# Moving the S5 blocks' rows between partitions by DMA through DRAM, in a two-layer decoder trunk on one core

## The chip, the cores and the metric

The kernel runs on one core of a Trainium2 chip. The metric is the time of one execution on the device in microseconds (us). The kernel before took 1357.15 us (median of three runs, 1355.7 to 1358.05). A profile is one execution recorded by the hardware profiler. Its engines are TensorE (PE, with its weight loads as PEld), VectorE (DVE), ScalarE (ACT), GpSimd (POOL) and SyncE (SP). "SPq" and "ACTq" are DMA issues by SP and ACT.

## The reference, cut to what matters

One sequence of 512 tokens, width 1024, passes two layers; each has a token mixer and a SwiGLU feed-forward part. The first layer's mixer has two branches on the same normalised input, an S5 state space and an HGRN2 recurrence, whose outputs are concatenated and projected. Only the S5 branch is touched:

```python
uf = u.reshape(bsz, seq, S5_GROUPS, 16)             # 32 groups of 16 channels, 64 complex states each
bu = einsum('gph,blgh->blgp', b_bar, uf)
_, states = associative_scan(combine, (a, bu), axis=1)       # state_t = lam_bar * state_{t-1} + bu_t
y = einsum('ghp,blgp->blgh', c_mat, states).real + d_skip * uf
y = gelu(y.reshape(bsz, seq, 512))
y_a = y * sigmoid(y @ w_glu + b_glu)                 # S5 branch
y_b = hgrn2_mixer(hq, hf, hi, hg, ...)               # four heads of 128
mixed = concatenate([y_a, y_b]) @ ev_w_out
```

## The kernel before

All activations lie with channels on the 128 partitions and the 512 tokens along the free dimension. Products are made with fp32 split into a high and a low float32r part (`split`, `wsplit`: an ACT copy makes the high part, a subtraction on DVE the low part) and three matmuls for each pair (`proj`, lines 275 to 277). Weights come by SP's DMA queue into three "raw" buffers. The adaLN products (`ada_run`) run beside all this: SP loads pieces of `ada_w` into two "ar" buffers, and DVE adds each to `acc` (L202, L204); these additions keep their program order on DVE, and `pace` says how many go with each weight load.

The S5 branch has 512 channels, in four blocks of 128 (`s5_block(q, ...)`, q = 0 to 3). Its input is `ups[q]`, the projection `u`, which lies in PSUM, in one of four "mm" buffers; the same four buffers serve the later projections. The block takes four consecutive tokens at a time, so that the recurrence steps over 128 groups of four. For that, rows have to change partition. U[32r..32r+31, j, n] (r = 3 - s) is channel 32j..32j+31 of token 4n + s: token phase s moves to a quarter of the partitions, and channel quarter j moves to the free dimension. Sixteen DVE copies of 32 partitions by 128 do this (L775). Then PE makes `vps` from `U` (L780), DVE and POOL rotate it (the tiles `rz0a` to `rz0d`, with q as the digit), DVE scans (L792), both rotate back, and PE makes `yp` (L804 to L806), again with token phases on the partition quarters. Sixteen ACT copies of 32 by 128 put `yp` back into channel order as `yf`.

`s5_next()` calls one block, and then `s5_mats(q + 1)` prepares the next block's matrices: products on POOL, copies into zeroed tiles on ACT, small transposes on PE. The four calls stand between the HGRN2 heads' projections (`hg_fq`, `hg_v`, `hg_g`: tiles hq, hf, hk, lg, hv, hg) and their recurrence cores (`core`: tiles e_h, sc_h, tot_h, lv_h). When all four `yf` are there, `gelu()` runs on each in place and `s5_glu` splits them, multiplies by `s5_w_glu`, and gates (`ys`). ACT's functions that need a table run in program order (`tact`), so the sigmoids of head 3 come after the last gelu.

Working tiles come from pools with tags, each with a number of slots: "s" has 16, "X" 4, "r" 8. Five "s" slots stay with the zeroed tiles. `U` takes an "X" slot for q below 3 and an "s" slot for q = 3; `yf` takes an "r" slot. The order of the instructions on each engine is not the written one: a planner chooses it, by the priority of the program order and its own costs, when a tile's slot and inputs are there. At run time each engine goes through its list in order.

Of the kernel before, what the change touches and what calls it, by code (L numbers as in the profile page):

```python
# [8 lines left out]
F32 = mybir.dt.float32  # L9
# [4 lines left out]
AF = mybir.ActivationFunctionType  # L14
ALU = mybir.AluOpType
AX = mybir.AxisListType

P = 128
D = 1024
T = 512  # L20
# [21 lines left out]
def trunk(  # L42
# [8 lines left out]
    nc = tc.nc  # L51
    x = x[0]
    out = out[0]

    cp = ctx.enter_context(tc.tile_pool(name="cp", bufs=1))
    wp = ctx.enter_context(tc.tile_pool(name="wp", bufs=3))
    xp = ctx.enter_context(tc.tile_pool(name="xp", bufs=1))
    hp = ctx.enter_context(tc.tile_pool(name="hp", bufs=2))
    tp = ctx.enter_context(tc.tile_pool(name="tp", bufs=1))
# [5 lines left out]
    def tt(name, tag, shape=(P, T), dtype=F32):  # L65
        return tp.tile(list(shape), dtype, tag=tag, name=name, bufs=SLOTS[tag])
# [7 lines left out]
    def mm_ps(name, shape=(P, T)):  # L74
        return pm.tile(list(shape), F32, tag="mm", name=name)
# [4 lines left out]
    def ps_b(name, shape=(P, T)):  # L80
        return pa.tile(list(shape), F32, tag="b", name=name)

    V, A, G, PE = nc.vector, nc.scalar, nc.gpsimd, nc.tensor

    def act(o, i, f, **kw):
        return A.activation(out=o, in_=i, func=f, **kw)  # L86
# [4 lines left out]
    def tact(o, i, f, **kw):  # L91


        def queue(new):
            if table["last"] is not None:
                tc.add_manual_dep(new.ins, table["last"].ins.name, order, reason="table sets in order")
            table["last"] = new

        if table["set"] != TABLES[f]:
            table["set"] = TABLES[f]  # L100
            queue(A.preload_act_table_set(TABLES[f]))
        ins = act(o, i, f, **kw)
        queue(ins)
        return ins

    def ttv(e, o, a, b, op):
        e.tensor_tensor(out=o, in0=a, in1=b, op=op)  # L107
# [133 lines left out]
    def wraw(src, nk, name, cols=P):  # L241
        raw = wp.tile([P, nk, cols], F32, tag="raw", name=f"raw_{name}", bufs=3)
        nc.sync.dma_start(out=raw, in_=src.rearrange("(k p) n -> p k n", p=P))
        return raw

    def wsplit(raw, nk, name, cols=P, e=nc.vector):
        hi = wp.tile([P, nk, cols], F32R, tag="whi", name=f"whi_{name}", bufs=3)
        act(hi, raw, AF.Copy)
        lo = wp.tile([P, nk, cols], F32R, tag="wlo", name=f"wlo_{name}", bufs=3)
        ttv(e, lo, raw, hi.bitcast(F32), ALU.subtract)  # L250
        return hi, lo
# [3 lines left out]
        ada_steps()  # L255
        return w

    def split(e, src, name, th, tl):
        hi = tt(f"hi_{name}", th, dtype=F32R)
        lo = tt(f"lo_{name}", tl, dtype=F32R)  # L260
        act(hi, src, AF.Copy)
        ttv(e, lo, src, hi.bitcast(F32), ALU.subtract)
        return hi, lo

    def blocks(w, cols=slice(0, P)):
# [3 lines left out]
    def proj(ps, ws, acts, ts=slice(0, T), ks=None):  # L269

        n = len(ws)
        for i, ((hi, lo), (ah, al)) in enumerate(zip(ws, acts, strict=True)):
            if ks and i not in ks:
                continue
            PE.matmul(ps, lhsT=hi, rhs=ah[:, ts], start=(i == 0), stop=False)  # L275
            PE.matmul(ps, lhsT=hi, rhs=al[:, ts], start=False, stop=False)  # L276
            ins = PE.matmul(ps, lhsT=lo, rhs=ah[:, ts], start=False, stop=(i == n - 1))  # L277
        return ins
# [467 lines left out]
    def s5_tables(q):  # L746
# [15 lines left out]
        tact(ph, ph, AF.Sin, scale=TWO_PI)  # L762
        return cosT, ph

    def s5_block(q, uT, mats, rot):

        rho = prm[3]
        Km, Wn, (Wr, Wi) = mats
        cosT, sinT = rot
        shp = [P, 4, P]  # L770
        U = tt(f"U{q}", "X" if q < 3 else "s", (P, 4, P))
        for j in range(4):
            for s in range(4):
                r = 3 - s
                V.tensor_copy(out=U[32 * r : 32 * r + 32, j, :], in_=uT[32 * j : 32 * j + 32, s:T:4])  # L775
        vps = []
        for i in range(2):
            ps = ps_b(f"vps{q}{i}", (P, 4, P))
            for j in range(4):
                PE.matmul(ps[:, j, :], lhsT=Wn[i][:, j, :], rhs=U[:, j, :], start=True, stop=True)  # L780
            vps.append(ps)
        t = [tt(f"rz{q}{z}", "s", shp) for z in "abcd"]
        ttv(V, t[0], vps[0], cosT, ALU.mult)
        ttv(V, t[1], vps[1], sinT, ALU.mult)
        ttv(V, t[2], vps[1], cosT, ALU.mult)
        ttv(V, t[3], vps[0], sinT, ALU.mult)
        ttv(V, t[0], t[0], t[1], ALU.add)
        ttv(G, t[2], t[2], t[3], ALU.subtract)
        z = [t[1], t[3]]
        for i in range(2):  # L790
            for j in range(4):
                V.tensor_tensor_scan(  # L792
                    out=z[i][:, j, :], data0=rho[:, q * 4 + j : q * 4 + j + 1].to_broadcast([P, P]),
                    data1=t[2 * i][:, j, :], initial=0.0, op0=ALU.mult, op1=ALU.add)

        ttv(V, t[0], z[0], cosT, ALU.mult)
        ttv(G, t[2], z[1], sinT, ALU.mult)
        ttv(V, t[0], t[0], t[2], ALU.subtract)
        ttv(V, z[0], z[0], sinT, ALU.mult)
        ttv(G, z[1], z[1], cosT, ALU.mult)  # L800
        ttv(V, z[0], z[0], z[1], ALU.add)
        yp = ps_b(f"yp{q}", (P, 4, P))
        for j in range(4):
            PE.matmul(yp[:, j, :], lhsT=Km[:, j].rearrange("p t c -> p (t c)"), rhs=U[:, j, :], start=True, stop=False)  # L804
            PE.matmul(yp[:, j, 1:], lhsT=Wr[:, j, :], rhs=t[0][:, j, 0 : P - 1], start=False, stop=False)
            PE.matmul(yp[:, j, 1:], lhsT=Wi[:, j, :], rhs=z[0][:, j, 0 : P - 1], start=False, stop=True)  # L806
        yf = tt(f"yf{q}", "r")
        for j in range(4):
            for s in range(4):
                act(yf[32 * j : 32 * j + 32, s:T:4], yp[32 * s : 32 * s + 32, j, :], AF.Copy)  # L810
        return yf

    def s5_glu(yf):
        wg = []
        for i in range(2):
            w = wsplit(wraw(s5_w_glu[0, i * 2 * P : (i + 1) * 2 * P, :], 2, f"wg{i}", T), 2, f"wg{i}", T, V)
            wg += [tuple(z[:, k, :] for z in w) for k in range(2)]
        yr = [split(V, y, f"yr{k}", "s", "s") for k, y in enumerate(yf)]
        res = []
        for m in range(4):  # L820
            ps = mm_ps(f"glu{m}")
            proj(ps, [tuple(z[:, m * P : (m + 1) * P] for z in w) for w in wg], yr)
            y = tt(f"ys{m}", "s")
            tact(y, ps, AF.Sigmoid, bias=cols2[:, 12 + m : 13 + m])
            ttv(G, y, y, yf[m], ALU.mult)
            res.append(split(V, y, f"ys{m}", "s", "s"))
        return res


    def ffn(l, h, then):  # L830
# [4 lines left out]
        for part, n in enumerate((12, 10)):  # L835
            gs = []
            for t in range(t0, t0 + n):
                pace[:] = 2 * int(part > 0 or t > 1), 10
                cs_ = slice(t * P, (t + 1) * P)
                ups = []  # L840
                for i, w in ((1, w1), (3, w3)):
                    w = wload(w[:, cs_], KT, f"f{i}_{l}{t}")
                    ups.append(((mm_ps if t else (ps_a, ps_b)[i // 3])(f"f{i}_{l}{t}"), blocks(w)))
                    if t:
                        proj(*ups[-1], h)
                if not t:
                    proj_halves(ups, h)
                (pa_, _), (pb_, _) = ups
                g = tt(f"g{l}{t}", "n")
                tact(g, pa_, AF.Silu)  # L850
                ttv(V, g, g, pb_, ALU.mult)
                gs.append(split(V, g, f"g{l}{t}", "s", "t"))
# [210 lines left out]
    def s5_next():  # L1063
        q = len(yfs)
        yfs.append(s5_block(q, ups[q], mats[q], rot[q]))
        if q < 3:
            mats.append(s5_mats(q + 1))
# [21 lines left out]
    pace[0] = 8  # L1089
    g1 = hg_g(1)  # L1090
    ys = s5_glu(yfs)
    in_step(hg_core(2, os[2], fq2, v1, ps_a), hg_core(3, os[3], fq3, v1, ps_b))
    heads += hg_outs(hg_out(2, os[2], g1, ps_a), hg_out(3, os[3], g1, ps_b))
# [48 lines left out]
    for hd in range(4):  # L1142
        ps = mm_ps(f"ga2{hd}")
        PE.matmul(ps, lhsT=a2r[:, hd * P : (hd + 1) * P], rhs=ga[0:96, :], start=True, stop=True)
        tag, pst = (("s", ps_b), ("t", ps_a))[hd % 2]
# [110 lines left out]
```

## Time and profile before

| | us |
|---|---|
| median of three runs | 1357.15 |
| profiled execution | 1364.62 |
| its span, first to last instruction | 1362.8 |
| PE busy | 1286.2 (94%) |
| DVE busy | 797.2 (58%) |
| ACT busy | 487.5 (36%) |
| POOL busy | 151.0 (11%) |

The span is what the trace covers; 1.8 us lie around it. The S5 blocks run between about 90 and 280 us. Whole-span shares average that stretch with a long feed-forward part behind it, so the stretch has to be read by itself. In a timeline row the first number is the start, the second the length, and a bracket at the end is the time for which the engine stood idle before it, with what released it.

### The profile page before, as it was taken

The page shows a single profiled execution, that of the slowest core. Times are in us where ns is not written, and L with a number is a line of the kernel's source. Part 1 is how long each engine was busy: PE and PEld are TensorE (multiplying, and loading weights), DVE is VectorE, ACT ScalarE, POOL GpSimd, SP SyncE. Part 2 cuts the span into 40 slices and gives each one's busy share as a digit, 9 for nine tenths or more (in the row PEclk, how much of TensorE's full clock was granted, in tenths as well). Part 3 has the DMA queues.
Part 4 walks back from the last instruction along what each step waited for, and adds up shares of the span by engine and source line. Part 5 has one row for each costly group of instructions (what it writes and reads, how often), then busy time and mean ns, then how long its engine had stood idle before and what let it go on. Part 6 is the DMA issues. An engine that isn't in the chain of part 4 may idle for free.

```text
span 1362.8 us, 18262 instructions
## 1 busy us (share of the span) xinstructions
PE 1286.2 (94%) x6949; PEld 1103.4 (81%) x6949; DVE 797.2 (58%) x1511; ACT 487.5 (36%) x851; POOL 151.0 (11%) x148
## 2 busy tenths in 40 slices
PE   6598899799899999999999999999899999999997
PEld 3377887778888888888889999998788888888886
DVE  4979796887865566665445446557653333333344
ACT  5253556423532322222334434432442322232232
POOL 1764451120100000000000000000100000000000
PEclk9779998889899999999999999999999999999999
DMA  8624540534067768987333232213223323433222
GB/s 293 163 63 129 150 140 16 126 94 132 18 142 188 202 174 213 214 219 198 106 106 94 65 92 63 74 49 97 62 82 104 93 74 103 117 93 93 79 86 83
DMA packets 222824, 159.69 MB, mean 117 GB/s; under 512 B 16752, under 2 KB 195248, under 8 KB 222736
## 3 DMA queue, kind: packets, MB, share of 16 engines
q1 hardware_dynamic: 221696, 157.48, 42.2%
q10 hardware_dynamic: 1040, 1.05, 0.3%
q8 instruction: 54, 0.88, 0.3%
q14 instruction: 34, 0.28, 0.1%
HBM read 156.40 MB, written 2.10 MB: 116 GB/s over the span
## 4 chain that ended last, share of the span: by engine, by line
PE 78%; DVE 12%; DMA 4%; ACT 2%; issue 2%; POOL 1%; SPq 0%; DVEq 0%; ACTq 0%
PE f L275 18%; PE f L276 18%; PE f L277 18%; DMA ar<-in_ada_w_dram 3%; PE op L276 2%; PE op L275 2%; PE op L277 2%; PE lv_g L465 2%; DVE acc L204 2%; PE gr L300 1%; PE gr L301 1%; PE gr L299 1%; PE gv L301 1%; PE gv L300 1%; PE gv L299 1%
## 5 line engine op out<-in xcount | busy, mean ns | idle before, releaser
L276 PE MATMUL f<-hlo_f,whi_f 128*128 128x512 f32 (+1 forms) x736 | 281.5, 383 | 0.2 <-DVE hlo_f L116 0.2
L275 PE MATMUL f<-hhi_f,whi_f 128*128 128x512 f32 (+1 forms) x736 | 280.9, 384 | 0.5 <-ACT hhi_f L86 0.5
L277 PE MATMUL f<-hhi_f,wlo_f 128*128 128x512 f32 (+1 forms) x736 | 280.8, 382 | 0.0
L86 ACT ACTIVATE whi_f<-raw_f 128x1024 fp32r<-128x1024 f32 x88 | 93.3, 1061 | 307.0 <-PE f L276 169.3
L107 DVE TENSOR_TENSOR wlo_f<-raw_f,whi_f 128x1024 fp32r<-128x1024 f32 x88 | 107.7, 1224 | 115.1 <-ACT whi_f L86 114.8
L276 PEld LDWEIGHTS f<-hlo_f,whi_f 128*128 128x128 f32 x736 | 140.1, 190 | 27.0 <-DVE hlo_f L116 0.8
L275 PEld LDWEIGHTS f<-hhi_f,whi_f 128*128 128x128 f32 x736 | 139.8, 191 | 27.0 <-ACT hhi_f L86 1.0
L277 PEld LDWEIGHTS f<-hhi_f,wlo_f 128*128 128x128 f32 x736 | 140.1, 191 | 26.5
L204 DVE SCALAR_TENSOR_TENSOR acc<-ar,cond,acc 128x512 f32<-128x512 f32 x154 | 120.1, 780 | 41.6 <-DMA ar<-in_ada_w_dram 40.0
L277 PE MATMUL f<-hi_g,wlo_c 128*128 128x512 f32 x312 | 121.7, 390 | 0.0
L276 PE MATMUL f<-lo_g,whi_c 128*128 128x512 f32 x312 | 121.6, 390 | 0.0
L275 PE MATMUL f<-hi_g,whi_c 128*128 128x512 f32 x312 | 121.2, 390 | 0.0
L86 ACT ACTIVATE whi_c<-raw_c 128x768 fp32r<-128x768 f32 (+1 forms) x56 | 44.9, 801 | 161.8 <-PE f L276 114.1
L107 DVE TENSOR_TENSOR g<-g,f 128x512 f32<-128x512 f32 x44 | 30.3, 688 | 109.3 <-PE f L277 109.3
L107 DVE TENSOR_TENSOR wlo_c<-raw_c,whi_c 128x768 fp32r<-128x768 f32 (+1 forms) x56 | 50.3, 898 | 57.6 <-ACT whi_c L86 57.5
L276 PEld LDWEIGHTS f<-lo_g,whi_c 128*128 128x128 f32 x312 | 58.6, 188 | 12.1
L275 PEld LDWEIGHTS f<-hi_g,whi_c 128*128 128x128 f32 x312 | 58.6, 188 | 12.1
L277 PEld LDWEIGHTS f<-hi_g,wlo_c 128*128 128x128 f32 x312 | 58.6, 188 | 12.1
L116 DVE SCALAR_TENSOR_TENSOR x<-f,mod,x 128x512 f32<-128x512 f32 (+1 forms) x36 | 24.8, 689 | 39.4 <-PE f L277 39.2
L107 POOL TENSOR_TENSOR na_m<-na_m,nsq_m 128x256 f32<-128x256 f32 x7 | 5.7, 818 | 365.3 <-DMA raw_c<-in_ffn_w_dram 337.9
L300 PE MATMUL gv<-wlo_gv,hhi_m 128*128 128x256 f32 x128 | 36.7, 287 | 0.0
L301 PE MATMUL gv<-whi_gv,hlo_m 128*128 128x256 f32 x128 | 36.6, 286 | 0.0
(667 smaller groups left out, 2677.9 us busy)
## 6 DMA issues: line engine op xcount, KB each, us to landing
raw_f<-in_ffn_w_dram SPq DMA_DIRECT2D x88, 512.0 KB, 3.8
ar<-in_ada_w_dram SPq DMA_DIRECT2D x256, 128.0 KB, 3.7
ar<-in_ada_w_dram SPq DMA_DIRECT2D x64, 256.0 KB, 5.3
raw_c<-in_ffn_w_dram SPq DMA_DIRECT2D x32, 384.0 KB, 3.5
raw_c<-in_ffn_w_dram SPq DMA_DIRECT2D x24, 320.0 KB, 3.2
raw_gv<-in_od_w_in_dram SPq DMA_DIRECT2D x8, 512.0 KB, 4.4
raw_gr<-in_od_w_in_dram SPq DMA_DIRECT2D x8, 512.0 KB, 4.0
raw_o<-in_ev_w_out_dram SPq DMA_DIRECT2D x8, 384.0 KB, 3.4
```

Source lines behind the costliest of these rows:

```text
L86: return A.activation(out=o, in_=i, func=f, **kw)
L107: e.tensor_tensor(out=o, in0=a, in1=b, op=op)
L116: V.scalar_tensor_tensor(out=o, in0=a, scalar=s, in1=b, op0=op0, op1=op1)
L204: ins = V.scalar_tensor_tensor(out=acc, in0=w, scalar=c_, in1=acc, op0=ALU.mult, op1=ALU.add)
L275: PE.matmul(ps, lhsT=hi, rhs=ah[:, ts], start=(i == 0), stop=False)
L276: PE.matmul(ps, lhsT=hi, rhs=al[:, ts], start=False, stop=False)
L277: ins = PE.matmul(ps, lhsT=lo, rhs=ah[:, ts], start=False, stop=(i == n - 1))
L299: PE.matmul(o, lhsT=ah[:, s], rhs=hi, start=(k == 0), stop=False)
L300: PE.matmul(o, lhsT=ah[:, s], rhs=lo, start=False, stop=False)
L301: PE.matmul(o, lhsT=al[:, s], rhs=hi, start=False, stop=(k == KT - 1))
L465: PE.matmul(ps[0:nk, w, :].rearrange("p (n b) -> p n b", b=b), lhsT=K[:, w * P : w * P + nk], rhs=qv[:, w * nb : (w + 1) * nb, b:], start= ...
```

## The change

A helper `quarters` writes a tile of 128 partitions by 4 by 128 to a DRAM scratch with one DMA, issued by ACT, and reads it back with four DMAs of 32 partitions each, issued by POOL. Both sides move rows of 128 fp32 numbers (512 bytes). For the input, four ACT copies per block first put `u` from PSUM into a tile `ud` of 128 partitions, with the tokens in order of phase, and `quarters` makes `U` from it. For the output, one ACT copy puts `yp` into a tile `yo`, and `quarters` makes `yd`, which takes the place of `yf`. `yd` holds the tokens ordered by phase, and what reads it (`gelu`, the split of `yr`, the gate on `ys`) reads it through a view with the tokens in order again, in steps of 128 numbers. `ud` and `yo` take "s" slots; `U` and `yd` take the slots that `U` and `yf` had.

```diff
+    dp = ctx.enter_context(tc.tile_pool(name="dp", bufs=1, space=bass.MemoryType.DRAM))
...
-    def split(e, src, name, th, tl):
+    def split(e, src, name, th, tl, view=lambda z: z):
         hi = tt(f"hi_{name}", th, dtype=F32R)
         lo = tt(f"lo_{name}", tl, dtype=F32R)
-        act(hi, src, AF.Copy)
-        ttv(e, lo, src, hi.bitcast(F32), ALU.subtract)
+        act(view(hi), src, AF.Copy)
+        ttv(e, view(lo), src, view(hi.bitcast(F32)), ALU.subtract)
         return hi, lo
...
+    def quarters(name, dst, src):
+
+        dr = dp.tile([4, P, P], F32, name=f"q_{name}", tag=f"q_{name}")
+        nc.scalar.dma_start(out=dr.rearrange("b p n -> p b n"), in_=src)
+        for b in range(4):
+            nc.gpsimd.dma_start(out=dst[32 * b : 32 * b + 32], in_=dr[b].rearrange("(a c) n -> c a n", c=32))
+
     def s5_block(q, uT, mats, rot):
...
+        ud = tt(f"ud{q}", "s", (P, 4, P))
+        for s in range(4):
+            act(ud[:, 3 - s, :], uT[:, s:T:4], AF.Copy)
         U = tt(f"U{q}", "X" if q < 3 else "s", (P, 4, P))
-        for j in range(4):
-            for s in range(4):
-                r = 3 - s
-                V.tensor_copy(out=U[32 * r : 32 * r + 32, j, :], in_=uT[32 * j : 32 * j + 32, s:T:4])
+        quarters(f"U{q}", U, ud)
...
-        yf = tt(f"yf{q}", "r")
-        for j in range(4):
-            for s in range(4):
-                act(yf[32 * j : 32 * j + 32, s:T:4], yp[32 * s : 32 * s + 32, j, :], AF.Copy)
-        return yf
+        yo = tt(f"yo{q}", "s", (P, 4, P))
+        act(yo, yp, AF.Copy)
+        yd = tt(f"yd{q}", "r", (P, 4, P))
+        quarters(f"y{q}", yd, yo)
+        return yd.rearrange("p s n -> p n s")
...
-        yr = [split(V, y, f"yr{k}", "s", "s") for k, y in enumerate(yf)]
+        yr = [split(V, y, f"yr{k}", "s", "s", lambda z: z.rearrange("p (n s) -> p n s", s=4)) for k, y in enumerate(yf)]
...
-            ttv(G, y, y, yf[m], ALU.mult)
+            ttv(G, y.rearrange("p (n s) -> p n s", s=4), y.rearrange("p (n s) -> p n s", s=4), yf[m], ALU.mult)
```

## Rows read from the trace of the kernel before

**Rows 1.** The page's busy times, and the granted clock by slices.

```profile
PE 1286.2 (94%) x6949; PEld 1103.4 (81%) x6949; DVE 797.2 (58%) x1511; ACT 487.5 (36%) x851; POOL 151.0 (11%) x148
...
PEclk9779998889899999999999999999999999999999
```

**Rows 2.** Busy time by stretch: length, engines (instructions), granted clock, DMA share, GB/s.

```profile
90.00:110.00 20.00, 20.00 (x113) 17.24 (x112) 19.17 (x56) 9.00 (x18) 0.58 (x1) 1.00 0.36 106
110.00:150.00 40.00, 32.48 (x206) 29.38 (x206) 31.27 (x53) 19.38 (x45) 24.06 (x16) 0.94 0.55 153
150.00:200.00 50.00, 45.15 (x341) 43.61 (x340) 48.42 (x83) 23.11 (x50) 22.98 (x16) 0.94 0.49 131
200.00:230.00 30.00, 27.82 (x169) 23.89 (x167) 17.38 (x33) 14.95 (x38) 9.90 (x5) 0.89 0.11 36
230.00:300.00 70.00, 57.86 (x328) 52.15 (x327) 62.11 (x142) 33.06 (x70) 13.96 (x9) 0.85 0.43 107
...
345.00:1362.80 1017.80, 997.80 (x5312) 861.17 (x5310) 522.71 (x931) 332.47 (x528) 27.10 (x29) 0.99 0.42 113
```

**Rows 3.** The chain of waits in the 215 us from 85 to 300.

```profile
by line: DMA ar<-in_ada_w_dram 11.9%; DVE acc L204 9.7%; issue 8.5%; DVE U L775 6.6%; POOL rz0c L107 3.4%; DVE e_h L107 3.2%; ACT yf L86 2.7%; SPq L188 2.4%; PE lv_h L465 2.3%; DVE wlo_hq L107 1.9%; DVE tot_h L107 1.9%; DVE sc_h L479 1.7%; 
```

**Rows 4.** The tiles U and yf: durations in ns (min/median/max), first and last start.

```profile
L775 DVE COPY U<-u x64: 271/286/298, 89.8 to 236.3; 32x128 f32<-32x128 f32 x64
...
L86 ACT ACTIVATE yf<-yp x64: 382/391/403, 139.7 to 265.1; 32x128 f32<-32x128 f32 x64
```

**Rows 5.** DVE's timeline: copies of U, and the second block's first rotation.

```profile
89.84 4.80 DVE L775 COPY U<-u 32x128 f32<-32x128 f32 x16 [5.92 <-PE u L277]
...
108.01 2.12 DVE L775 COPY U<-u 32x128 f32<-32x128 f32 x7
...
154.16 0.68 DVE L107 TENSOR_TENSOR rz1a<-vps,cos 128x512 f32<-128x512 f32 x1
...
229.36 0.55 DVE L113 TENSOR_SCALAR lg<-lg,lbm 128x512 f32<-128x512 f32 x1 [8.78 <-ACT lg L86]
...
230.99 1.48 DVE L775 COPY U<-u 32x128 f32<-32x128 f32 x5
...
233.26 3.35 DVE L775 COPY U<-u 32x128 f32<-32x128 f32 x11
```

**Rows 6.** PE's timeline: the products from U, first and last.

```profile
103.68 1.05 PE L780 MATMUL vps<-U,wn 128*128 128x128 f32 x8
...
236.66 1.38 PE L780 MATMUL vps<-U,wn 128*128 128x128 f32 x10 [0.76 <-DVE U L775]
```

**Rows 7.** ACT's timeline around the last two blocks' outputs.

```profile
219.63 6.38 ACT L86 ACTIVATE yf<-yp 32x128 f32<-32x128 f32 x16
...
228.73 0.59 ACT L86 ACTIVATE lg<-hf 128x512 f32<-128x512 f32 x1
...
259.06 6.43 ACT L86 ACTIVATE yf<-yp 32x128 f32<-32x128 f32 x16 [1.84 <-PE yp L806]
...
267.14 0.64 ACT L86 ACTIVATE yf<-yf 128x512 f32<-128x512 f32 x1
...
278.45 0.33 ACTq L1134 DMA_DIRECT2D ng<-in_gla_norm_g_dram  x1
```

**Rows 8.** Who waited for whom, 85 to 300 us: total, times, longest.

```profile
DVE acc L204 <- DMA ar<-in_ada_w_dram: 10.6, 5, 4.2
```

**Rows 9.** The tiles Kz, wn and rz0d: nearest rows for added work.

```profile
L86 ACT ACTIVATE Kz<-s5M x24: 305/308/312, 102.6 to 227.9; 32x128 f32<-32x128 f32 x24
...
L86 ACT ACTIVATE wn<-wnp x8: 581/598/602, 96.3 to 233.9; 128x512 f32<-128x512 f32 x8
...
L107 POOL TENSOR_TENSOR rz0c<-rz0c,rz0d x1: 7254/7254/7254, 115.3 to 115.3; 128x512 f32<-128x512 f32 x1
...
L107 POOL TENSOR_TENSOR rz0d<-rz0d,cos x1: 1262/1262/1262, 126.3 to 126.3; 128x512 f32<-128x512 f32 x1
```

**Rows 10.** DMA: a queue's packets, MB, share; issues with KB each, us to landing.

```profile
q1 hardware_dynamic: 221696, 157.48, 42.2%
...
ar<-in_ada_w_dram SPq DMA_DIRECT2D x256, 128.0 KB, 3.7
...
out_dram<-ob ACTq DMA_DIRECT2D x2, 256.0 KB, 2.8
...
cidx<-in_cst_dram ACTq DMA_DIRECT2D x1, 64.0 KB, 2.4
```

## The prediction, made before the changed kernel was run

> **What bounds the kernel now.** I read the busy times first [rows 1]: PE is busy 94% of the span, so over the whole kernel only PE's gaps and its slow stretches can be won. Next the busy time by stretch [rows 2]. Behind 345 us PE works 997.80 of 1017.80 us at a clock of 0.99, and nothing there is touched: whatever is won or lost before 300 us moves that part as a whole. The S5 stretch, 90 to 300 us, is another matter. PE has no gap from 90 to 110, but idles 40 - 32.48 = 7.5 us from 110 to 150, 4.9 us from 150 to 200, 2.2 us from 200 to 230, and 70 - 57.86 = 12.1 us from 230 to 300: 26.7 us in all. DVE is nearly full in the same stretches (19.17 of 20, then 48.42 of 50, then 62.11 of 70), so the reader is to see two engines near their limit, with DVE feeding PE.
>
> Third comes the chain of waits over the 215 us from 85 to 300 [rows 3]. It runs mostly over DVE and the transfers that DVE waits for: 11.9% is the landing of `ar` pieces (25.6 us), 9.7% the `acc` additions, 6.6% the copies of `U` (14.2 us), 2.7% the ACT copies of `yf` (5.8 us). So the copies that go away are on the path, 20 us of them. That is a bound on the gain, not the gain: when a link goes, the next latest takes over, and PE's idle time of 26.7 us also holds waits that this change does not touch.
>
> **What the change removes.** DVE loses 64 copies of 0.286 us [rows 4], 18.3 us: 48 of them (13.7 us) are for blocks 0 to 2, the first sixteen at 89.84 us in one run of 4.80 us, and the last sixteen stand at 231 to 236.6 us, 1.48 + 3.35 = 4.8 us [rows 5]. ACT loses 64 copies of 0.391 us, 25.0 us [rows 4].
>
> **What it adds.** ACT gets sixteen copies of 128 by 128 (`ud`). No row has this shape with a stepped PSUM source; the bounds are 0.308 us (a 32 by 128 copy) [rows 9] and 0.391 us (a copy with stepped output) [rows 4], and I take 0.35, midway: 5.6 us. Four `yo` copies of 128 by 512 at 0.598 us [rows 9] are 2.4 us. Eight DMA issues at 0.33 us [rows 7] are 2.6 us. So ACT gets 10.6 us for 25.0 us removed, and is 14.4 us lighter.
>
> POOL gets 32 DMA issues. The trace has none by POOL. The bounds are 0.33 us, an issue by ACT [rows 7], and 7.25 us, the longest POOL operation, `rz0c`, which ran beside a full DVE [rows 9]. I take 1.2 us, near a POOL operation of its usual length (1.262 us for `rz0d`) [rows 9], since what POOL does for a transfer is more like a small operation than like ACT's issue: 38 us. In front of each four issues POOL also waits for ACT's write to land, 0.33 + 2.8 us (a 256 KB store) [rows 7, 10], eight times: 25 us. Together 63 us, beside 210 - 71.5 = 138.5 us in which POOL is idle from 90 to 300 (the sum of its column in [rows 2] is 71.5). It fits, and I cost it at nothing. The cover is gone if the waits stand in front of POOL's rotations; that is the second rival.
>
> The DMA engines get 4.2 MB: each of eight moves writes 256 KB and reads it, 512 + 512 packets of 512 bytes, 8192 in all. On queue q1 a packet took 0.422 x 16 x 1362.8 / 221696 = 41.5 ns of one engine [rows 10], so 8192 of them take 21 us of all sixteen, a tenth of the 210 us, on top of shares of 0.11 to 0.55 [rows 2]. DVE waits 10.6 us in this stretch for `ar` transfers [rows 8]. Ends: nothing, and 2 us if the waits grow by a fifth, twice the added load; I take 1 us.
>
> Latency. The move of `U` takes 4 x 0.35 + 0.33 + 2.8 us for the write, then 4 x (0.33 to 1.2) and 2.4 us (a 64 KB transfer) [rows 10] for the reads: 8.3 to 11.7 us, where sixteen copies took 4.80 us. From 89.84 us on, `U0` is there at 98.1 to 101.6 us; PE first uses it at 103.68 us [rows 6]. It is covered by 2 us or more, by other projections on a full PE. `U1` and `U2` have more room: the last copies of `U2` ended at 110.1 us, and the second block's rotation came only at 154.16 us [rows 5]. `U3` can be made any time after its projection has ended, if the planner has an "s" slot for it.
>
> **The sum.** (a) From 110 to 200 us PE idles 12.4 us, in which DVE is late; it starts 13.7 us lighter. Ends: nothing, when the `ar` transfers hold it at the old pace, and the whole 12.4 us. I take 5 us, below the middle, because the transfers are the longest part of the chain [rows 3]. (b) The copies of `yf2` hold ACT at 219.63 us for 6.38 us, `lg` comes only at 228.73 us [rows 7], and DVE stands 8.78 us for it [rows 5]. PE has other work there and idles 2.2 us in the stretch: ends 0 and 2.2, I take 1.5 us. (c) `U3` is on the chain for 4.8 us, and PE waits for it (0.76 us directly) [rows 6]; the 12.1 us of idle PE from 230 to 300 can take that up. Ends 0 and 4.8; I take 4 us. (d) `y3` gets later. It starts at 259.06 us and was done at 265.5 us; gelu took it at 267.14 us [rows 7]. By DMA it lands at 259.06 + 0.6 + 0.33 + 2.8 + 4 x (0.33 to 1.2) + 2.4 = 266.5 to 270.0 us. Against 267.14 that is a gain of 0.6 us to a loss of 2.9 us; the sigmoids of head 3 wait behind it on ACT. I take 2 us lost. (e) The transfers cost 1 us, as above. The stepped views of `yd` change no count of elements; I cost them at nothing, and the cover is the same engines' slack.
>
> Sum: 5 + 1.5 + 4 - 2 - 1 = 7.5 us. The profiled execution took 1364.6 us (span 1362.8 and 1.8 around it), so its like would take 1357.1 us. The median of the runs, 1357.15 us, lies 7.5 us under the profiled one, and the same gain from it gives about **1349.6 us**. The ends of the terms give a gain of 12.4 + 2.2 + 4.8 + 0.6 = 20 us (1337 us) and a loss of 2.9 + 2 = 4.9 us (1362 us).
>
> **Rivals.** First, the full lead. DVE and ACT are ahead by all that is taken off, and the fourth "mm" buffer, held by `u3` until 236 us, comes free early, so projections start sooner. For it speaks that DVE has almost no idle time from 90 to 200 us; against it that PE itself has none until 110. It gives up to 20 us, 1337 us; I put it at 1340 us.
>
> Second, on the other side, POOL becomes the gate. POOL takes its list in order, and a read that waits for a landing (3.1 us, and four issues of 1.2 us: 7.9 us) holds the rotation queued behind it; `rz0c` was on the chain for 7.3 us already [rows 3]. If that happens to three of the blocks' rotations it costs 3 x 7.9 = 23.7 us, and less the 7.5 us won the time is 1357.15 + 16 = 1373 us. It decides from the point where the added waits on the path pass 7.5 us, that is, one move in front of a rotation that DVE is waiting for. For it speaks that a POOL operation stretched from 1.262 to 7.254 us beside a full DVE [rows 9], so POOL cannot be counted on. Against it: POOL is idle for two thirds of the stretch, 138.5 of 210 us [rows 2].
> The Trainium skill speaks against the change here: its page "SBUF — State Buffer", section "SBUF: two separate sides", says that the descriptors of a POOL-issued DMA are written by GpSimd, which VectorE locks out of a shared SBUF port while it runs an operation that takes both ports; it advises the ACT or SP queue instead. By that the reads would be late by VectorE's operations, and the second rival's time would hold. Its section "Who interferes with whom" says that a subtraction of two tensors, which is most of DVE's work here, blocks only what GpSimd reads, not what it writes; by that the starvation is short and the sum stands. No row here shows a POOL-issued DMA.
>
> Third, nothing is won: the `ar` transfers (25.6 us of the chain) set DVE's pace, and the copies were only what DVE did meanwhile. Then (a) and (c) are gone, and (b), (d) and (e) leave a loss of 1.5 us: 1358.7 us, within 2.7 us of before. For it speaks the 10.6 us of waits [rows 8]; against it that DVE is at 95% and more in two of the stretches [rows 2].
>
> **How the numbers follow.** The forecast (a gain of 3 to 13 us) gets 0.45, the full lead 0.15, no gain 0.18, POOL as the gate 0.22. A measurement of this kernel can tell about 0.2% (2.7 us) from no change. So faster is 0.60, the same 0.18, slower 0.22. The likeliest case alone spans 1344 to 1354 us. The range is 1337 to 1364 us: it holds the full lead's end and nothing won, and leaves out most of the POOL case, some 0.17, and a little below.
>
> **What would show it.** Right: from 110 to 200 us PE's idle time falls below 8 us; `U3` is there well before 230 us; DVE's wait for `lg` shrinks; the issues on POOL are near 1.2 us, and its rotations start when DVE's inputs are there. Wrong: PE or DVE waiting for POOL's `rz` tiles or for transfers of `U` and `yd`, landings far over 3 us, or the `ar` waits growing by as much as the copies gave. The span behind 345 us should keep its length; if it moves by more than 3 us, the comparison is of something else.

## The result: 38 us slower

The changed kernel took 1395.84 us (median of 4 runs, 1394.2 to 1399.0), the kernel before 1357.60 us beside it (4 runs, 1355.7 to 1362.3). The ratio is 1.0279, 95% interval 1.0246 to 1.0312: slower, where 1349.6 us was forecast, and far over the range of 1337 to 1364 us. The profiled execution took 1394.2 us, 29.6 us more than the profiled one of before (1364.6 us, itself 7 us over the median); what follows explains those 29.6 us by rows, and the medians by runs.

First the page of the changed kernel, its busy times and the granted clock by slices [rows 1].

```profile
PE 1289.7 (93%) x6949; PEld 1107.8 (80%) x6949; DVE 786.7 (56%) x1447; ACT 471.7 (34%) x807; POOL 150.8 (11%) x180
...
PEclk9789997859999999999999999999989999999999
```

ACT is 15.8 us lighter, near the 14.4 us forecast. DVE is 10.5 us lighter, less than the 18.3 us of its copies: `lo_yr`, which now reads in steps, takes 2 us more, and the rest of the gap was not traced. PE is busy 3.5 us longer; its idle time is span less busy, 102.7 us against 76.6 before. So 26.1 of the 29.6 us are PE waiting. Where it waits shows in the busy time by stretch [rows 2]: length, PE, PEld, DVE, ACT, POOL, granted clock, DMA share, GB/s.

```profile
90.00:110.00 20.00, 15.86 (x81) 12.82 (x80) 10.63 (x16) 8.89 (x22) 2.35 (x4) 1.00 0.85 214
110.00:150.00 40.00, 33.20 (x208) 30.71 (x209) 27.17 (x36) 9.02 (x16) 15.43 (x19) 0.91 0.53 137
150.00:200.00 50.00, 46.66 (x331) 44.10 (x331) 40.75 (x54) 16.57 (x34) 20.02 (x20) 0.97 0.57 157
...
230.00:300.00 70.00, 39.87 (x236) 36.22 (x235) 45.66 (x107) 20.41 (x54) 24.39 (x29) 0.67 0.25 64
...
345.00:1392.40 1047.40, 1027.99 (x5490) 886.84 (x5488) 544.28 (x978) 343.31 (x553) 27.32 (x29) 0.99 0.41 114
```

PE had no gap from 90 to 110 us and now has 4.1 us; from 230 to 300 it idles 30.1 us (12.1 before), and the granted clock there is 0.67 of 2.4 GHz (0.85 before). But DVE isn't full any more either: 10.63 of 20 us, 45.66 of 70. Both engines wait for something else. The last row has grown by 29.6 us, and only because work was pushed into it (5490 matmuls, 5312 before): the first product `f` of the feed-forward part starts at 394.5 us instead of 366.6, 27.9 us later, and from there to the end it is 997.9 us against 996.2.

What is late shows on two timelines. ACT's: start, length, form, and in brackets the idle time before it.

```profile
99.24 0.60 ACT L87 ACTIVATE wn<-wnp 128x512 f32<-128x512 f32 x1 [1.22 <-PE wnp L741]
99.74 0.78 ACT L87 ACTIVATE ud<-u 128x128 f32<-128x128 f32 x4
...
156.34 0.57 ACT L87 ACTIVATE wn<-wnp 128x512 f32<-128x512 f32 x1
156.82 0.72 ACT L87 ACTIVATE ud<-u 128x128 f32<-128x128 f32 x4
...
261.29 0.79 ACT L87 ACTIVATE ud<-u 128x128 f32<-128x128 f32 x4
```

Before, `U0` to `U2` were made between 89.84 and 110.1 us [rows 5]. Now each `ud` comes right behind the last weights `wn` of its own block: `ud0` at 99.74 us, `ud1` at 156.82 us, `ud3` at 261.29 us. And POOL's timeline:

```profile
106.00 2.35 POOL L771 DMA_DIRECT2D U<-q_U  x4 [25.07 <-DMA q_U<-ud]
...
130.08 2.10 POOL L108 TENSOR_TENSOR B1a<-s5b,s5L 128x256 f32<-128x256 f32 x2
...
163.03 2.17 POOL L771 DMA_DIRECT2D U<-q_U  x4 [21.24 <-DMA q_U<-ud]
...
183.51 1.43 POOL L108 TENSOR_TENSOR B2a<-s5b,s5L 128x256 f32<-128x256 f32 x2
```

`B1a` and `B2a` are the first matrices of the next block. POOL made them at 83.33 and 131.26 us before; now at 130.08 and 183.51, some 50 us later. They lead, by `Bd0z` (ACT), `M` and `wnp` (PE) and `Kz` and `wn` (ACT), to the block's rotation. At the first step behind POOL, ACT's copy `Bd0z`, 27 and 38 us of this are left (111.3 and 158.0 us before, 138.3 and 195.6 now). The start of the chain between 150 and 172 us (start, length) shows how the two meet:

```profile
151.35 0.31 ACT Kz L87
...
156.43 0.48 ACT wn L87
156.91 0.64 ACT ud L87 x4
...
157.57 4.92 DMA q_U<-ud
...
163.03 1.62 POOL U L771 x3
164.66 3.75 DMA U<-q_U
...
168.55 3.04 PE vps L789 x16
```

The block's last matrix, then `ud`, then 11.7 us to the first product from `U` (156.82 to 168.55), and PE waits. Before, `U` had long been there when the matrices came.

### The profile page after: what moved, and what is told of

It reads as the page before. It is cut to its first block, busy times and chain, and to the rows that moved or that the text cites. A ratio compares the mean times of both kernels' runs of the same rounds, so it can differ in the third digit from the quotient of the medians.

```text
span 1392.4 us, 18240 instructions
## 1 busy us (share of the span) xinstructions
PE 1289.7 (93%) x6949; PEld 1107.8 (80%) x6949; DVE 786.7 (56%) x1447; ACT 471.7 (34%) x807; POOL 150.8 (11%) x180
## 4 chain that ended last, share of the span: by engine, by line
PE 80%; DVE 8%; DMA 7%; ACT 2%; issue 2%; SPq 1%; POOL 0%; DVEq 0%; ACTq 0%; POOLq 0%
PE f L276 17%; PE f L277 17%; PE f L278 17%; DMA ar<-in_ada_w_dram 4%; PE op L276 2%; PE op L277 2%; PE op L278 2%; PE lv_g L466 2%; PE gr L301 1%; PE gr L302 1%; PE gr L300 1%; PE gv L302 1%; PE gv L301 1%; PE gv L300 1%; DVE acc L205 1%
## 5 line engine op out<-in xcount | busy, mean ns | idle before, releaser
L278 PEld LDWEIGHTS f<-hi_g,wlo_c 128*128 128x128 f32 x312 | 58.6, 188 | 12.1
L276 PEld LDWEIGHTS f<-hi_g,whi_c 128*128 128x128 f32 x312 | 58.6, 188 | 12.1
L466 PEld LDWEIGHTS lv_h<-e_h,hk 128*127 128x127 f32 (+6 forms) x224 | 27.8, 199 | 11.5 <-issue 7.4
L466 PE MATMUL lv_h<-e_h,hk 128*127 128x64 f32 (+6 forms) x224 | 28.7, 281 | 8.8 <-DVE sc_h L480 6.0
```

The costliest lines, as they stand in the source:

```text
L466: PE.matmul(ps[0:nk, w, :].rearrange("p (n b) -> p n b", b=b), lhsT=K[:, w * P : w * P + nk], rhs=qv[:, w * nb : (w + 1) * nb, b:], start= ...
```

## The experiments

Eighteen kernels were run. In the expectations S stands for the theory that late slots make the loss, L for the round trip, A for `ar` transfers that eat the gain, V for the stepped views, P for POOL. The table has sixteen of them by median, beside before and the changed kernel; the other two leave work out and stand under theory A. `B2a` and `rz3a` are where the profile shows the start of that matrix on POOL and of the last rotation. They come from one execution each, which can lie some us off the median (before: 1364.6 us, ud_n_yo_r: 1357.1, nr_sp: 1343.0).

| kernel | U, y by DMA | ud | yo | reads by | `B2a` | `rz3a` | us | ratio to before |
|---|---|---|---|---|---|---|---|---|
| nr_sp | both | n | r | SP | 127.5 | 213.7 | 1340.5 | 0.9864 [0.9850, 0.9878] |
| nr_act | both | n | r | ACT | 128.2 | 212.5 | 1342.0 | 0.9888 [0.9873, 0.9903] |
| y_sp | y | | r | SP | 130.4 | 218.3 | 1346.6 | 0.9919 [0.9904, 0.9934] |
| U_sp | U | n | | SP | 125.6 | 223.1 | 1347.6 | 0.9923 [0.9909, 0.9937] |
| pool_waits | both | n | r | SP | 147.1 | 227.3 | 1354.9 | 0.9972 [0.9956, 0.9988] |
| yo_r_sp | both | s | r | SP | 133.1 | 230.4 | 1357.7 | 0.9993 [0.9973, 1.0012] |
| before | none | | | | 131.3 | 238.9 | 1357.6 | |
| U_only_n | U | n | | POOL | 134.5 | 242.3 | 1358.4 | 1.0008 [0.9995, 1.0020] |
| views_only | none | | | | 129.3 | 232.5 | 1359.1 | 1.0000 [0.9988, 1.0013] |
| ud_n_yo_r | both | n | r | POOL | 146.5 | 234.7 | 1362.4 | 1.0017 [1.0001, 1.0033] |
| y_only_r | y | | r | POOL | 147.0 | 237.4 | 1365.3 | 1.0045 [1.0013, 1.0076] |
| before_U_s | none | | | | 134.2 | 226.8 | 1367.6 | 1.0068 [1.0048, 1.0087] |
| ud_n | both | n | s | POOL | 177.8 | 251.8 | 1371.5 | 1.0096 [1.0068, 1.0124] |
| ud_n_sp | both | n | s | SP | 169.2 | 249.9 | 1372.3 | 1.0103 [1.0081, 1.0124] |
| y_only_s | y | | s | POOL | 180.5 | 256.7 | 1374.0 | 1.0126 [1.0111, 1.0142] |
| U_only_s | U | s | | POOL | 157.0 | 268.9 | 1387.0 | 1.0215 [1.0193, 1.0236] |
| sp_reads | both | s | s | SP | 178.6 | 273.6 | 1391.9 | 1.0248 [1.0232, 1.0264] |
| changed | both | s | s | POOL | 183.5 | 272.2 | 1395.8 | 1.0279 [1.0246, 1.0312] |

Each ratio is to runs of before taken beside that kernel; their medians lie between 1357.0 and 1359.5 us.

**The slots.** Two letters of the changed kernel:

```diff
-        ud = tt(f"ud{q}", "s", (P, 4, P))
+        ud = tt(f"ud{q}", "n", (P, 4, P))
...
-        yo = tt(f"yo{q}", "s", (P, 4, P))
+        yo = tt(f"yo{q}", "r", (P, 4, P))
```

> The changed kernel with two letters different: `ud` takes its slot from tag "n" and `yo` from tag "r", instead of both from "s". All transfers, copies and views are the same. Theory S (slots): the 38 us come from `ud` and `yo` standing in line for "s" slots behind the tiles of the block's matrices, so that U1 and U2 were made at 163 and 216 us instead of by 110 us, and u1 to u3 held three of the four "mm" buffers meanwhile. S expects U1 and U2 to have landed by 115 us and the time to come back to 1345 to 1365 us. Rival L (latency and POOL's list): the cost is the round trip through DRAM, eight times 10 to 12 us of which part is exposed; nothing of it changes, so the time stays within 10 us of 1396 us. Rival V (the stepped views of yd and the load of the transfers): also within 10 us of 1396 us.

1362.4 us: 33 of the 38 us come back, as theory S said and L and V did not. With the first letter alone (ud_n):

> The changed kernel with only `ud` moved from tag "s" to tag "n"; `yo` stays in "s". Theory S: U0 to U2 land by 115 us, but the next block's matrices (B, W, wn) still stand behind yo in the line for "s", so they are made only after each block's output; the time lies between, 1360 to 1385 us. If it is the same as with both moved, yo's slot costs nothing. Rivals L and V: within 10 us of 1396 us.

1371.5 us: `ud` is worth 24 us, `yo` a further 9. Then the other way, before with `U0` to `U2` in "s", no DMA:

```diff
-        U = tt(f"U{q}", "X" if q < 3 else "s", (P, 4, P))
+        U = tt(f"U{q}", "s", (P, 4, P))
```

> The kernel before, without any transfer through DRAM, with one letter different: U0 to U2 take "s" slots as U3 does, instead of "X" slots. Theory S: the sixteen copies of U1 and U2 come late, as in the changed kernel, u1 and u2 hold their "mm" buffers, and the time is 1372 to 1395 us with no DMA in it at all. Rivals L and V: no transfer and no stepped view, so 1353 to 1362 us.

1367.6 us: a late `U` costs 9 us when sixteen copies of 4.8 us make it, less than expected. So the late slot alone is the smaller part of the 24 us that `ud` is worth.

**One side at a time.** y alone by DMA, yo in "r" (U by DVE copies, as before), then U alone with `ud` in "n" and in "s" (y by ACT copies, as before):

```diff
-        quarters(f"U{q}", U, ud)
+        for j in range(4):
+            for s in range(4):
+                r = 3 - s
+                V.tensor_copy(out=U[32 * r : 32 * r + 32, j, :], in_=uT[32 * j : 32 * j + 32, s:T:4])
```

> Only the output goes by DMA: the sixteen VectorE copies per block that make U are back, and `yo` takes an "r" slot. Theory S: no tile is added to the line for "s", so the time is near before, 1352 to 1366 us; what is left over is the price of y3's round trip (about 8 us against 6.4 us of copies, and then gelu) and of the stepped views. Rival L: half of the eight round trips remain, and the only one of the four that nothing covers, so 1370 to 1380 us. Rival V: the views are all there, so most of the 38 us stay, 1380 us or more.

> Only the input goes by DMA, with `ud` in tag "n"; the output's 64 ScalarE copies into yf are back, and with them the views in plain token order. Theory S+A (the slots cost the time; without them the `ar` transfers set the pace): VectorE is 18 us lighter and no cost of the output's side is left, but the waits for `ar` grow by most of what the copies gave, so 1350 to 1358 us. Rival F (the output's side ate the gain that I forecast): 1344 to 1350 us, all of the 7 us and more. Rival L (round trips): U0 to U2 land early but U3's trip is exposed, 1360 us or more.

> As the run before, but with `ud` in tag "s" as in the changed kernel; there is no yo. The kernel before with U in "s" and no DMA lost 9 us, and moving ud out of "s" in the changed kernel gained 25 us. Theory S x L (the slot makes U late, and only then is the round trip of 10 to 12 us, against 4.8 us of copies, on the path, once per block): 9 + 3 x 6 = 27 us over before, 1380 to 1390 us. Pure S (only the lateness counts): 1364 to 1370 us, as with the copies in "s".

1365.3, 1358.4 and 1387.0 us. The last fits the theory that the slot makes the round trip count. But the middle one gains nothing, with DVE 18 us lighter and no late slot. So the forecast gain went somewhere else as well.

**Theory A, the `ar` transfers.** DVE's waits for them had grown from 10.6 us [rows 8] to 19.6 us in ud_n_yo_r. Two kernels leave out loads of `ar` in the first three groups of layer 0:

```diff
+                if l or pieces[0] == 5 or not k:
                     wr = wp.tile([P, 2, T], F32, tag="ar", name=f"ar{l}{pieces[0]}{k}", bufs=2)
```

> The kernel before, leaving out the loads of ada_w for the first three groups of layer 0 but the first piece of each: VectorE does the same additions, from a piece that stays in its buffer, so the adaLN values of that layer are not the reference's. It takes the `ar` transfers out of the stretch from 90 to 280 us. Theory A: in the kernel before VectorE is the pace and waits 10.6 us for ar, so it gains 5 to 12 us: 1345 to 1353 us. Rival: these waits are covered, 1355 to 1360 us.

> The same loads left out of the kernel with both sides by DMA, ud in "n" and yo in "r" (1362 us with the loads, waits for ar 19.6 us, 38.9 us of the chain). Theory A: the ar transfers had taken the place of the copies, so without them this kernel gains more than the kernel before does, 15 to 25 us, and falls below it: 1335 to 1347 us, and the 5 to 10 us that I forecast appear between the two. Rival V (the output's views and the round trip of y3 ate it): it gains as much as the kernel before and stays level with it or above.

1348.3 us (0.9925 [0.9901, 0.9949]) for before and 1349.5 us (0.9939 [0.9918, 0.9960]) for ud_n_yo_r. Without the transfers the kernel with DMA gains 12.9 us and the one without 8.7 (by the ratios, 10.6 and 10.2); it is still no faster than that one, as rival V said. So some 4 us at most are `ar`'s, and theory A falls. (What follows shows that POOL held this kernel back as well.)

**Stepped views, and who issues the reads.** Four more, all on that question: before with `yf` laid out by phase and read by the stepped views; y alone with `yo` in "s"; and ud_n_yo_r with its 32 reads issued by SP, or by ACT (`nc.scalar`).

```diff
-            nc.gpsimd.dma_start(out=dst[32 * b : 32 * b + 32], in_=dr[b].rearrange("(a c) n -> c a n", c=32))
+            nc.sync.dma_start(out=dst[32 * b : 32 * b + 32], in_=dr[b].rearrange("(a c) n -> c a n", c=32))
```

> The kernel before, no DMA of U or y: only yf is laid out as yd is, so that the ACT copies write contiguous rows and hi_yr, lo_yr, ys and gelu use the stepped view. Theory V (the stepped views are what the y side costs): the sixteen stepped operations take 0.4 to 0.5 us more each as in the changed kernel, and the time is 1362 to 1367 us, as with y alone by DMA (5.7 us lost). Rival (the cost of the y side is the round trip of y3 and the wait behind it): 1355 to 1360 us, within 0.2% of before.

> y alone by DMA, with yo in the s slots as in the changed kernel; U by VectorE copies. Theory S (a late slot costs time by itself): yo's slot cost 9 us beside U by DMA (1371.5 against 1362.4), so 1365.3 + 9 = 1374 us, 1370 to 1378. Rival (the slot costs only when U is late as well): 1363 to 1368 us, as with yo in the r slots.

> Both moves by DMA with ud in n and yo in r (1362.4 us), the 32 reads issued by SP instead of POOL. Rival P (POOL's issues and waits cost the rest of the gain): POOL is free of 18 us of issues and some 25 us of waits, 1350 to 1357 us. Theory (latency and next-latest links, POOL hides its part): 1359 to 1367 us; the waits now stand in SP's list ahead of ar loads.

> The same with the 32 reads issued by ACT, right behind its own write of the scratch. Rival P (POOL's part costs): 1350 to 1357 us. Theory (POOL hides its part, ACT does not): each of eight moves holds ACT's list for the landing, 3.1 us, and four issues of 0.33 us, 4.4 us, 35 us in all, of which ACT's idle time hides more than half: 1365 to 1380 us.

Laid out by phase, `yf` costs nothing in all: 1359.1 against 1358.6 us. That is not the views alone, for the 64 copies of `yf` got shorter with it (391 to 268 ns, 7.9 us of ACT). `yo` in "s" costs 8.7 us with U made by copies too. And one word, the issuing queue, is worth 22 us (21 by the ratios): 1340.5 us with SP, 1342.0 with ACT. I had not expected it; my theory said 1359 to 1367. Rival P, POOL as the gate, pointed the right way, both kernels came out below its 1350 to 1357 us, and both beat the one before. Rows of nr_sp, busy time by stretch (columns as above):

```profile
110.00:150.00 40.00, 36.17 (x243) 33.98 (x242) 35.77 (x51) 18.23 (x37) 20.75 (x19) 0.91 0.76 194
150.00:200.00 50.00, 44.29 (x350) 43.17 (x349) 46.62 (x86) 15.51 (x37) 25.17 (x19) 0.93 0.41 112
200.00:230.00 30.00, 30.00 (x181) 25.42 (x179) 24.00 (x46) 19.74 (x31) 5.78 (x3) 1.00 0.26 80
230.00:300.00 70.00, 64.68 (x402) 56.85 (x402) 58.91 (x130) 24.68 (x47) 10.20 (x6) 0.98 0.49 126
```

PE idles 3.8, 5.7, 0 and 5.3 us where it idled 7.5, 4.9, 2.2 and 12.1 before. POOL's timeline tells why it differs from ud_n_yo_r, as far as two executions 14 us apart show the 22 us. First ud_n_yo_r:

```profile
92.17 2.35 POOL L771 DMA_DIRECT2D U<-q_U  x4 [11.04 <-DMA q_U<-ud]
...
102.40 2.12 POOL L108 TENSOR_TENSOR B1a<-s5b,s5L 128x256 f32<-128x256 f32 x2
...
144.28 2.19 POOL L771 DMA_DIRECT2D yd<-q_y  x4 [15.06 <-DMA q_y<-yo]
146.48 1.90 POOL L108 TENSOR_TENSOR B2a<-s5b,s5L 128x256 f32<-128x256 f32 x2
...
155.28 1.28 POOL L108 TENSOR_TENSOR rz1c<-rz1c,rz1d 128x512 f32<-128x512 f32 x1
...
195.58 1.27 POOL L108 TENSOR_TENSOR rz2c<-rz2c,rz2d 128x512 f32<-128x512 f32 x1
```

Then the same of nr_sp:

```profile
82.46 1.83 POOL L108 TENSOR_TENSOR B1a<-s5b,s5L 128x256 f32<-128x256 f32 x2
...
127.50 1.30 POOL L108 TENSOR_TENSOR B2a<-s5b,s5L 128x256 f32<-128x256 f32 x2 [1.56 <-DVE rz0b L108]
...
146.35 1.29 POOL L108 TENSOR_TENSOR rz1c<-rz1c,rz1d 128x512 f32<-128x512 f32 x1 [7.85 <-DVE rz1d L108]
...
179.95 1.76 POOL L108 TENSOR_TENSOR rz2c<-rz2c,rz2d 128x512 f32<-128x512 f32 x1
```

With the reads on POOL, `B1a` stands behind the reads of `U` and comes 20 us later; `B2a` stands behind the read of `y0`, for which POOL waited 15.06 us, and comes 19 us later. The rotation stands behind it in turn: `rz1c` follows without idle time, 6.4 us after the rotation's first product on DVE (148.86 us), where nr_sp has 2.6 us (143.79); for `rz2c` it is 10.7 us (from 184.84) against 3.7 (from 176.26). The late `B1a` does not reach the next step: ACT copies it (into `Bd0z`) at 110.2 us in ud_n_yo_r and at 114.5 in nr_sp. `B2a` and `B3a` are copied 7 and 17 us later than in nr_sp (147.4 and 181.0 us, shown below), and the last rotation starts 21 us later. The tile Bd0z in ud_n_yo_r (ns min/median/max, first and last start):

```profile
L87 ACT ACTIVATE Bd0z<-B1a x2: 412/414/417, 110.2 to 110.6; 64x256 f32<-64x256 f32 x2
L87 ACT ACTIVATE Bd0z<-B2a x2: 417/418/420, 154.7 to 155.1; 64x256 f32<-64x256 f32 x2
L87 ACT ACTIVATE Bd0z<-B3a x2: 413/416/420, 197.6 to 198.0; 64x256 f32<-64x256 f32 x2
```

In the 215 us from 85 to 300 POOL of ud_n_yo_r waited, by the view of waits (total, times, longest):

```profile
POOL yd L771 <- DMA q_y<-yo: 55.5, 4, 16.7
...
POOL U L771 <- DMA q_U<-ud: 11.6, 2, 11.0
```

**POOL's order or POOL's DMAs?** nr_sp with a POOL operation of 32 by 1 behind each move: the wait stands in POOL's list again, without a DMA. Beside it the changed kernel with nothing altered but the queue of the reads, and each side alone on SP.

```diff
             nc.sync.dma_start(out=dst[32 * b : 32 * b + 32], in_=dr[b].rearrange("(a c) n -> c a n", c=32))
+        pw = cp.tile([P, 1], F32, name=f"pw_{name}", tag=f"pw_{name}")
+        ttv(G, pw[0:32], dst[0:32, 0, 0:1], dst[0:32, 0, 0:1], ALU.mult)
```

> nr_sp (1340.5 us; reads on SP) with one tiny POOL operation behind each of the eight moves, which reads one column of the first 32 rows of U or yd: POOL's list has the wait again, about as long as the reads held it, but no DMA issue. Theory Q (POOL loses by the order of its list: what is queued behind the wait comes late): 1355 to 1365 us, most of the 22 us lost again. Rival D (it loses by issuing DMAs, 17.6 us of issue, or by later landings): 1338 to 1346 us.

> The changed kernel with its 32 reads issued by SP instead of POOL, ud and yo still in the s slots. If POOL and the slots add up, POOL's 22 us come off 1395.8: 1370 to 1378 us. Rival (a late slot alone makes the loss, whoever issues the reads): 1388 to 1397. Rival (POOL's list is nearly the whole cost, late slots cost only the 10 us that they cost with copies): 1345 to 1356.

> U alone by DMA, ud in n, reads on SP; y by the ACT copies of before. With the reads on POOL it was 1358.4, no gain. If POOL ate the gain of the U side: 1344 to 1352 us. If the gain of nr_sp comes from the y side: 1355 to 1360 us.

> y alone by DMA, yo in r, reads on SP; U by the VectorE copies of before. With the reads on POOL it was 1365.3, 5.7 us slower than before. POOL waited 54 us for the four y moves there: without that wait, 1350 to 1358 us. If y's own round trip or its stepped views cost the 5.7 us: 1362 to 1367 us.

pool_waits took 1354.9 us, at the lower edge of theory Q, which is the order of POOL's list (D is its DMAs): with no DMA issued by POOL, 14.4 of the 22 us are lost again (15 of 21 by the ratios). POOL is held about as long, by 87 us of waits where ud_n_yo_r has 70 us of waits and 17.6 us of issues. Its timeline has the same wait and the same late matrix:

```profile
146.84 0.30 POOL L108 TENSOR_TENSOR pw_y<-yd 32x1 f32<-32x1 f32 x1 [16.66 <-DMA yd<-q_y]
...
147.10 1.20 POOL L108 TENSOR_TENSOR B2a<-s5b,s5L 128x256 f32<-128x256 f32 x2
```

The other 7.5 us (6 by the ratios) go with the issues on POOL or with where exactly the waits stand; which, no run tells. U_sp and y_sp gain 10.6 and 11.5 us: each side was a gain, and POOL ate both; y_sp came out below its expectation. But sp_reads took 1391.9 us, only 4 less than the changed kernel, against my 1370 to 1378: where the slots are late, POOL costs next to nothing. The two are not additive. With the reads on SP, the slots one at a time:

```diff
-        yo = tt(f"yo{q}", "r", (P, 4, P))
+        yo = tt(f"yo{q}", "s", (P, 4, P))
```

> nr_sp (1340.5 us) with only yo back in the s slots; ud stays in n. If yo's slot costs what it cost with the reads on POOL (8.6 to 9 us): 1348 to 1352 us. If yo's slot alone lets the s queue run late for the next blocks: 1360 to 1385.

> nr_sp (1340.5 us) with only ud back in the s slots; yo stays in r. If ud's slot is what makes the loss (29 us with U alone by DMA and the reads on POOL, more from a faster start): 1370 to 1385 us. If both slots are needed together: 1345 to 1360.

1372.3 us with `yo` in "s" and 1357.7 us with `ud` in "s" (that second kernel has the other letter changed): 32 and 17 us, together 49 of the 51 us between nr_sp and sp_reads. `yo`, which I had put at 9 us, is the larger; `ud`, which I had put at 29 us or more, is the smaller, and its kernel lies in the range of the rival that wants both slots together; but the two costs add up. The tile Bd0z in nr_sp, ACT's copies of the next blocks' matrices (ns min/median/max, first and last start):

```profile
L87 ACT ACTIVATE Bd0z<-B1a x2: 412/414/416, 114.5 to 115.0; 64x256 f32<-64x256 f32 x2
L87 ACT ACTIVATE Bd0z<-B2a x2: 407/412/417, 147.4 to 147.8; 64x256 f32<-64x256 f32 x2
L87 ACT ACTIVATE Bd0z<-B3a x2: 414/416/417, 181.0 to 181.4; 64x256 f32<-64x256 f32 x2
```

And in ud_n_sp:

```profile
L87 ACT ACTIVATE Bd0z<-B1a x2: 405/410/414, 137.4 to 137.8; 64x256 f32<-64x256 f32 x2
L87 ACT ACTIVATE Bd0z<-B2a x2: 399/406/414, 185.0 to 185.4; 64x256 f32<-64x256 f32 x2
L87 ACT ACTIVATE Bd0z<-B3a x2: 402/408/415, 236.4 to 236.8; 64x256 f32<-64x256 f32 x2
```

With `yo` in the row for an "s" slot, the next block's matrices (which are "s" tiles too, and come after `yo` in the program) are 23, 38 and 55 us later. From the chain of ud_n_sp behind the first of them (start, length): the matrix's products, then, without another wait for `U`, the products for the rotation.

```profile
143.78 0.13 PE M L722 x2
...
152.14 0.44 PE wnp L741 x4
...
153.29 0.89 PE vps L789 x8
```

That is also the likely reason why POOL's waits cost nothing there: ud_n and ud_n_sp differ by 0.8 us. Both mechanisms hold back the same things, the next block's matrices first. `B2a` comes at 169 to 178 us by the slot and at 146 to 147 by POOL, and the later one counts.

## Why the prediction was wrong, point by point

**The step that failed** is the working of what the change adds. It priced `ud` and `yo` by their copies (5.6 and 2.4 us of ACT) and never by the "s" slots that they take; of slots it says only that "`U3` can be made any time after its projection has ended, if the planner has an "s" slot for it". Measured with POOL out of the way, the two slots cost 51 us (1340.5 to 1391.9): 32 for `yo`, because the next block's matrices then get theirs later, and 17 for `ud`, because each `U` is then made only behind its own block's matrices. By medians it adds up: 17 us won (1357.6 to 1340.5), 51 lost by the slots, and 4 by the issues on POOL (1391.9 to 1395.8) make the loss of 38. "`U1` and `U2` have more room" held for the place where the copies had stood (110.1 us), not for tiles in another tag: `ud1` came at 156.82 us. The code shows what was needed to see it: 16 slots, five taken for good, and the matrices, `wn` and the rotations in the same tag.

**POOL, "it fits, and I cost it at nothing".** Wrong by 22 us once the slots are repaired (1362.4 against 1340.5), and hidden behind the slots in the changed kernel itself (4 us). I compared 63 us of work with 138.5 us of idle time; what counts is the place in the list. The second rival had the right mechanism: rotations queued behind the wait, and, which it did not name, the next block's matrices ahead of them. That its 23.7 us are near the 22 is partly luck: it reckoned with three waits of 7.9 us, and in ud_n_yo_r POOL waited 55.5 us for four moves of `y` alone. Nor was it this that put the changed kernel at 1395.8 us, where the rival's time was 1373. An issue took 0.55 us, not 1.2; tile U of the changed kernel (ns min/median/max, first and last start):

```profile
L771 POOL DMA_DIRECT2D U<-q_U x16: 548/551/714, 106.0 to 266.9; - x16
```

The Trainium skill, page "SBUF — State Buffer", section "SBUF: two separate sides", advises another queue for such DMAs because VectorE can starve GpSimd of the port for descriptors. The advice was right once the slots are repaired (22 us), but these traces don't show its reason: the issues hardly vary, 548 to 714 ns, and in ud_n_yo_r the reads of `yd` landed sooner from POOL than from SP in nr_sp (2.1 and 2.9 us). The reads of `U` landed later (7.1 against 3.0 us), beside a VectorE that was busy 10.9 of 20 us from 90 to 110; whether a wait for descriptors is in that, no run tells. My reading beside it, that subtractions are most of DVE's work, was wrong: before, from 90 to 300 us, the splits' subtractions took some 33 of its 178 us, and the additions to `acc` 39.

**The gain, terms (a) to (c)**, 10.5 us of the sum. They exist in nr_sp, in another split: PE idles 9.5 us from 110 to 200 (12.4 before; 2.9 won for 5 forecast), nothing from 200 to 230 (2.2; 2.2 for 1.5) and 5.3 from 230 to 300 (12.1; 6.8 for 4), 11.9 us in all. What the sum had no term for is the slow stretch: from 230 to 300 the granted clock is 0.98 for 0.85, and over the span PE is busy 9.2 us less (1286.2 to 1277.0). The 18 us gained are the first rival's 1340 us almost to the digit; that kernel has two letters and a word that the rival did not have, and the rival's argument that DVE has almost no idle time from 90 to 200 us was wrong from 110 to 150, where it is busy 31.27 of 40 us [rows 2]. So I count it as luck. In the changed kernel none of it shows: DVE waits there, and is busy 45.66 of 70 us.

**Latency.** The total was right, 11.7 us from `ud1` to the product, the upper end of 8.3 to 11.7, but by errors that cancel: the copies took 0.7 us for 1.4 and the four issues 2.2 for 4.8, while the write with its issue took 4.9 us for 3.1 and the last read 3.2 us to land for 2.4. Its cover was wrong, as above, for `U0` too: `ud0` came at 99.74 us where I reckoned from 89.84, and its first product at 111.3 us instead of 103.68.

**(d), `y3` later.** In nr_sp `yo3` starts at 234.74 us and gelu takes `yd3` at 247.1, 12.4 us, against 8.1 before (259.06 to 267.14): 4.3 us later for 2 forecast, and earlier in all, since the whole block is. In the changed kernel it is 9.1 us (290.97 to 300.1), 1.0 later.

**(e) and the views.** `ar` waits grew from 10.6 to 24.5 us in the changed kernel and to 15.4 in nr_sp, 4.8 for the 1 that I took; that they do not set the time is shown for ud_n_yo_r alone (no_ar_dma). The views' cost of nothing was not shown (views_only has the shorter copies beside it), and its reason was wrong: that no count of elements changes does not keep an operation's length. Tile yd of the changed kernel:

```profile
L87 ACT ACTIVATE yd<-yd x4: 1120/1140/1184, 203.0 to 300.1; 128x512 f32<-128x512 f32 x4
L87 ACT ACTIVATE hi_yr<-yd x4: 1077/1094/1135, 291.5 to 305.0; 128x512 fp32r<-128x512 f32 x4
L108 DVE TENSOR_TENSOR lo_yr<-yd,hi_yr x4: 1022/1066/1627, 297.5 to 315.0; 128x512 fp32r<-128x512 f32 x4
```

Gelu took 0.64 us before [rows 7], `hi_yr` 0.63 and `lo_yr` 0.68; now each is near 1.1 us.

**What stays open.** Why before_U_s, whose last rotation starts 12 us earlier than before's, ends 9 us later by the medians; the two profiled executions are only 2.7 us apart (1364.6 and 1367.3), so their rows cannot say. How much of the slots' cost is the "mm" buffers that `u` holds until `ud` is made: in the changed kernel PE waits 4.6 us for `ud` itself, and no run separates the rest. How the 24 us between ud_n and the changed kernel split between the slot of `ud`, the round trip and POOL's waits for `U` (59.4 us): with U alone the slot costs 29 us with POOL (1358.4 to 1387.0), with both sides on SP only 17.

## What to carry to other kernels

A new staging tile is priced by the slots of its tag first: who stands behind it in that tag, in program order, and what those tiles start. A wait that is added to an in-order queue is priced by what stands next in the list, not by the engine's idle total; another queue can be worth more than one that is idle on average (SP or ACT here, for POOL). Where a change that removes work comes out slower, put each added tile and each added issue elsewhere, one at a time, before giving the idea up: here two letters and one word turn a loss of 38 us into a gain of 18.

## What the runs showed of the hardware that I had not expected

Four reads of 64 KB issued by POOL took 2.17 to 2.35 us of its time, one 0.55 us. In the 215 us from 85 to 300 the reads of `U` landed in a median of 7.1 us from POOL (ud_n_yo_r) and 3.0 us from SP (nr_sp); those of `yd` in 2.1 and 2.9 us, and those of `U` in the changed kernel, from POOL, in 3.1, so the queue alone does not make the difference. Reading and writing fp32 in steps of 512 bytes took ACT 1.14 us for 128 by 512 elements (gelu, in place) where contiguous rows took 0.64, reading alone 1.09 for 0.63 (`hi_yr`), while ACT's 32 by 128 copies went from 391 ns [rows 4], with output in steps of 16 bytes, to 268 ns when their output became contiguous (views_only).
